# Layer 0's last MLP group summed in HBM, the weight sums of every MLP unit on VectorE, and later copies of running sums

## The chip, the cores and the metric

The kernel runs on one core of a Trainium2 chip. The metric is the device time of one launch in microseconds; the figure for the kernel before is the median of three runs, 2134.29 us (2131.2 to 2135.48).

## The reference

Two residual layers over 1024 tokens of width 1024, in fp32. Each layer adds a token mixer beside a 4-head cross-attention into 256 memory tokens, through one output projection, and then a squared-ReLU MLP of inner width 4096:

```python
for layer in range(2):
    h = rms_norm(x, norm_mix[layer])
    if layer % 2 == 0:
        y_mix, xq = rglru_group(h, w_in_a, ...)      # gated linear recurrence
    else:
        y_mix, xq = fox_group(h, w_in_b, ...)        # causal attention with forget gates
    y_mem = memory_group(xq, mem, norm_mem[layer], w_mem_kv[layer], ...)
    x = x + jnp.concatenate([y_mix, y_mem], axis=-1) @ w_out[layer]
    x = x + jnp.square(jax.nn.relu(rms_norm(x, norm_mlp[layer]) @ w_mlp_in[layer])) @ w_mlp_out[layer]
```

## The kernel before

Activations lie transposed, features on the 128 partitions, tokens along the free axis, in two halves of 512 tokens (h = 0 and h = 1). Every fp32 operand is split into a rounded part and a rest (`hi`, `lo`), and each product is three matmuls, hi*hi, hi*lo and lo*hi (`t3`). ScalarE writes `hi` (L316 for weights, L474 and L468 for activations), VectorE writes `lo` (L317, L477, L469). The residual stream x lies in HBM as `xs` (`xspill` in the trace) as eight blocks of 128 features.

The MLP of a layer runs in eight groups of 512 inner features. A group has two matrix products, `mlp_z` (first weight, w1) and `mlp_out` (second weight, w2), and each is done by a Winograd form of the 2x2 block product: seven block products instead of eight, in the order b11, b21, t2, t3, t1, t4, b22. Each is a call of `product` (matmuls at L1017, 24 of them on 512 columns). The price is sums of blocks. On the weight side these are a unit's S2 sums in `_wunit` (L355, L356, L357, twice each on 128x512, and L360 once on 128x1024), made on GpSimd, save that the first w1 unit of each layer makes them on VectorE (`u.dve = g == 0`). There are 8 w1 units and 8 w2 units in a layer.

On the activation side one PSUM bank collects several products in turn: A takes b11, then t2 on top of it, then t1, then b22; C takes t3 and then t4. A bank's running sum after b11, t2 and t3 is copied by ScalarE (`copies`, L1028) into an SBUF tile as soon as that product is done, and VectorE adds the other addend, another bank, when that is there (`plus`, L1033). In `mlp_z` the result goes through relu, scale and square (L1037, L1038), and combinations of the four blocks (L1138 to L1149) become operands of `mlp_out`. In `mlp_out` each of the 16 results of a group is added to `xs` in HBM by an accumulating DMA from GpSimd's queue (`send`, L1172).

The last group (g == 7) of both layers does otherwise: it reads x, adds it in SBUF, on GpSimd (L1192) or by an accumulating DMA into SBUF (L1195), and stores the finished x from SP's queue (`sink`, L1177). In layer 0 `sink` also squares the block for the next norm's statistics (`sqacc`, L438 and L444), and for h = 0 splits it for layer 1's projections (L468, L469). The key and value projection of layer 1's memory tokens (`kv`, matmuls at L385) starts before that group ends (two steps from `hook7`), and goes on after it.

All scratch tiles of 128x512 come from one set of 86 slots (`Slots`); the slot that was given back longest ago is taken first, and an instruction that writes a slot waits until its former reader, a DMA too, has ended. Weights go through four raw buffers and a ring of three split entries, `wnext` splitting up to three entries ahead. The order of the instructions on each engine is made at build time by a scheduler that goes by the program's order and its own model of durations.

In layer 1, groups 0 to 2 have their first two products done ahead (`mlp_park`) and read the results back, four tiles each, in the group before (`mlp_back`).

Of the kernel before, what the change touches and what calls it, by code (L numbers as in the profile page):

```python
# [175 lines left out]
class Builder:  # L176
# [712 lines left out]
    def outproj(self, h, ks, src, dst, gain, last, banks=("pj",)):  # L889
        nc = self.nc  # L890
        for m in range(8):
            x = self.load_x(m, h, src)
            wh, wl = self.wnext()
            ps = self.psum(banks[m % len(banks)])
            terms = []
            for i, k in enumerate(ks):
                c = slice(i * P, (i + 1) * P)
# [134 lines left out]
    def plus(self, f, ps):  # L1032
        self.nc.vector.tensor_tensor(f[:, :H], f[:, :H], ps, ALU.add)  # L1033

# [38 lines left out]
    def mlp_z(self, l, g, hook):  # L1073
# [19 lines left out]
        t, t2, w = [], [], []  # L1093
# [12 lines left out]
        else:  # L1106
            yield from run(A, "b11", True, self.copies(t))
            for o in range(2):
                hz[o]["b11"] = t[o]
# [43 lines left out]
    def mlp_out(self, l, g, mid):  # L1153
        nc = self.nc
        V, G = nc.vector, nc.gpsimd
        n = slice(0, H)
        hp = self.hp
        seen = set()
# [15 lines left out]

        def sink(f, q, a, b):
            x, dm = f[:, n], 2 * q + a
            nc.sync.dma_start((self.out if l else self.xs)[dm, :, b * H:(b + 1) * H], x)  # L1177
            if l == 0:
                self.sqacc(1 if b in seen else 0, b, x, V if b == 0 and a == 1 else None)
                seen.add(b)  # L1180
                if b == 0:
                    self.xg[0][dm] = self.split(x, self.pc("gmix1", dm))
            self.F.put(f)

        def keep(a, b):
            dst = []

            def first(q, ps):
                self.copies(dst)(q, ps)
                if g == 7 and a == b == 0:  # L1190
                    f = self.acc.pop(0)
                    G.tensor_tensor(dst[q][:, n], dst[q][:, n], f[:, n], ALU.add)  # L1192
                    self.F.put(f)
                elif g == 7:
                    nc.gpsimd.dma_start(dst[q][:, n], self.xs[2 * q + a, :, b * H:(b + 1) * H], accum_op=ALU.add)  # L1195

            def then(q, ps):
                self.plus(dst[q], ps)
                (sink if g == 7 else send)(dst[q], q, a, b)

            return first, then

        def end(q, ps):
            if g == 7:
                self.plus(acc[q], ps)
                sink(acc[q], q, 0, 1)
# [7 lines left out]
        c11, c21, c22 = keep(0, 0), keep(1, 0), keep(1, 1)  # L1214
# [576 lines left out]
```

## Time and profile before

| | |
|---|---|
| median of three runs | 2134.29 us |
| the profiled execution | 2132.37 us, its span 2130.7 us |
| TensorE matmul / weight load | 97% / 81% of the span |
| VectorE, ScalarE, GpSimd | 78%, 54%, 41% |
| mean granted TensorE clock | 0.988 of full speed |

The profile's page gives busy shares over the span; the table by stretch gives the same for windows, with the number of instructions (x), the granted clock, the share of the DMA engines and GB/s. A matmul record lasts longer than the distance to the next one, since matmuls are pipelined: 117 matmuls on 512 columns that start in 27 us are 0.231 us apart. In the views of waits each row has the engine and line that waited, what ended the wait, the us in total, the number of waits and the longest.

### The profile page before, as it was taken

How to read it: one execution, taken by the hardware profiler on the slowest of the kernel's cores; microseconds unless marked ns; L12 is line 12 of the kernel's file. 1: busy time of each engine (PE TensorE's matmuls, PEld its weight loads, DVE VectorE, ACT ScalarE, POOL GpSimd, SP SyncE). 2: the span in 40 equal slices, each digit the busy share in tenths (PEclk: the TensorE clock that was granted, in tenths of full speed). 3: DMA queues.
4: the chain of work that ended last, by engine and by line, in shares of the span. 5: the costliest groups of instructions: out<-in, count | busy, mean ns of one | idle time of the engine just before them, and what ended most of it. 6: DMA issues, size and time to landing. Idle time of an engine off the chain costs nothing. (4 is left out here: it accounts for less than half of the span.)

```text
span 2130.7 us, 30055 instructions
## 1 busy us (share of the span) xinstructions
PE 2071.5 (97%) x10466; PEld 1727.4 (81%) x10466; DVE 1663.3 (78%) x2708; ACT 1141.9 (54%) x2160; POOL 864.0 (41%) x844
## 2 busy tenths in 40 slices
PE   9999999999999999988999999999999999999998
PEld 8898878878778778767998998777777877787786
DVE  7988698877877877887677778776787768868777
ACT  6755655544454454555555646566544554445443
POOL 2222321535535525545342333422054645445444
PEclk8999999999999999989999999999999999999999
DMA  5422452546545635627768446934546675364474
GB/s 180 140 77 93 135 184 94 101 89 128 101 97 119 111 87 119 156 86 199 276 218 290 133 138 214 299 122 129 161 99 139 138 150 101 85 140 94 89 173 119
DMA packets 126392, 298.44 MB, mean 140 GB/s; under 512 B 14176, under 2 KB 16288, under 8 KB 126240
## 3 DMA queue, kind: packets, MB, share of 16 engines
q1 hardware_dynamic: 82464, 208.36, 29.4%
q0 software_dynamic: 43776, 88.17, 23.2%
q8 instruction: 82, 1.34, 0.3%
q14 instruction: 70, 0.57, 0.1%
HBM read 187.32 MB, written 109.15 MB: 139 GB/s over the span
## 5 line engine op out<-in xcount | busy, mean ns | idle before, releaser
L317 DVE TENSOR_TENSOR wl<-wr,wh 128x1024 fp32r<-128x1024 f32 (+2 forms) x362 | 441.2, 1229 | 108.5 <-ACT wh L316 104.1
L1017 PE MATMUL pspt<-r,wh 128*128 128x512 f32 x1536 | 485.1, 396 | 7.2 <-DVE r L477 2.6
L1172 POOL DMA_DIRECT2D xspill<-f x224 | 284.7, 1963 | 287.5 <-DVE f L1033 284.1
L316 ACT ACTIVATE wh<-wr 128x1024 fp32r<-128x1024 f32 (+3 forms) x411 | 306.0, 766 | 141.4 <-PE pss L1017 41.2
L1017 PEld LDWEIGHTS pspt<-r,wh 128*128 128x128 f32 x1536 | 289.0, 188 | 77.9 <-DVE r L477 4.3
L1017 PE MATMUL pss<-r,wh 128*128 128x512 f32 x1024 | 329.6, 400 | 19.8 <-ACT f L1028 8.1
L477 DVE TENSOR_TENSOR r<-f,r 128x512 fp32r<-128x512 f32 x282 | 230.1, 826 | 98.5 <-ACT r L474 39.9
L1017 PE MATMUL pspt<-r,wl 128*128 128x512 f32 x768 | 305.6, 398 | 0.2
L1017 PE MATMUL pspj<-r,wh 128*128 128x512 f32 x832 | 265.8, 399 | 2.1 <-DVE f L1033 1.0
L1017 PEld LDWEIGHTS pss<-r,wh 128*128 128x128 f32 x1024 | 192.6, 189 | 75.9 <-DVE r L477 13.9
L385 PE MATMUL pspj<-wh,r 128*128 128x256 f32 (+1 forms) x1280 | 248.5, 286 | 2.3 <-DVE r L1322 0.8
L474 ACT ACTIVATE r<-f 128x512 fp32r<-128x512 f32 x282 | 173.5, 626 | 106.2 <-DMA xspill<-f 49.0
L1038 ACT ACTIVATE f<-f 128x512 f32<-128x512 f32 x128 | 80.9, 632 | 269.5 <-DVE f L1037 269.4
L385 PEld LDWEIGHTS pspj<-wh,r 128*128 128x128 f32 x1280 | 201.6, 188 | 5.3 <-DVE r L1322 1.0
L1017 PE MATMUL pss<-r,wl 128*128 128x512 f32 x512 | 203.6, 398 | 0.0
L355 POOL TENSOR_TENSOR wr<-wr,wr 128x512 f32<-128x512 f32 x60 | 95.7, 1778 | 249.0 <-DVE wl L317 233.2
L1017 PEld LDWEIGHTS pspj<-r,wh 128*128 128x128 f32 x832 | 156.3, 189 | 39.4 <-DVE r L469 1.5
L385 PE MATMUL pspj<-wl,r 128*128 128x256 f32 (+1 forms) x640 | 181.1, 283 | 0.0
L1017 PEld LDWEIGHTS pspt<-r,wl 128*128 128x128 f32 x768 | 146.0, 190 | 36.9 <-DVE wl L317 2.0
L385 PE MATMUL pspj<-r,wh 128*128 128x512 f32 x488 | 164.1, 411 | 5.3 <-ACT r L474 2.1
L1017 PE MATMUL pspj<-r,wl 128*128 128x512 f32 x416 | 163.4, 397 | 0.6 <-DVE wl L317 0.5
L357 POOL TENSOR_TENSOR wr<-wr,f 128x512 f32<-128x512 f32 x60 | 135.4, 2550 | 17.1 <-issue 17.1
(301 smaller groups left out, 4035.3 us busy)
## 6 DMA issues: line engine op xcount, KB each, us to landing
wr<-in_w_dram SPq DMA_DIRECT2D x136, 512.0 KB, 4.5
xspill<-f POOLq DMA_DIRECT2D x224, 256.0 KB, 7.0
f<-xspill SPq DMA_DIRECT2D x88, 256.0 KB, 4.1
xspill<-f SPq DMA_DIRECT2D x64, 256.0 KB, 3.5
f<-in_xT_dram SPq DMA_DIRECT2D x32, 256.0 KB, 3.5
wr<-in_wkv_dram SPq DMA_DIRECT2D x16, 512.0 KB, 3.6
wr<-in_wina_dram SPq DMA_DIRECT2D x15, 512.0 KB, 3.6
wsp<-wh SPq DMA_DIRECT2D x14, 512.0 KB, 5.4
```

The source lines that it names most:

```text
L316: self.wact = self.nc.scalar.activation(hi, raw, AF.Copy)
L317: eng.tensor_tensor(lo, raw, hi.bitcast(F32), ALU.subtract)
L355: G.tensor_tensor(r["a11"][:, d], r["a11"][:, d], r["a21"][:, d], ALU.subtract)
L357: G.tensor_tensor(r["a12"][:, d], r["a12"][:, d], x, ALU.subtract)
L385: self.lastmm = self.nc.tensor.matmul(out, lhsT=a, rhs=b, start=(j == 0), stop=(j == n - 1))
L474: i = self.nc.scalar.activation(hi[:, :n], src, AF.Copy)
L477: self.nc.vector.tensor_tensor(lo[:, :n], src, hi[:, :n].bitcast(F32), ALU.subtract)
L1017: self.lastmm = self.nc.tensor.matmul(ps, lhsT=a, rhs=b, start=(start and c == 0 and j == 0), stop=(c == n - 1 and j == 2), skip_group_che ...
L1038: self.lastsq = self.nc.scalar.activation(f[:, n], f[:, n], AF.Square)
L1172: nc.gpsimd.dma_start(self.xs[2 * q + a, :, b * H:(b + 1) * H], f[:, n], accum_op=ALU.add)
```

## The change

Five edits, in one diff:

1. Every unit, w1 and w2, makes its S2 sums on VectorE.
2. Running sums are copied later. `both` copies one bank and adds the other at once, so that A after b11 is copied in b21's `done`, A after t2 in t3's, and C after t3 is not copied in `mlp_z` (VectorE reads it from PSUM in t1's `done`), and is copied in t1's `done` in `mlp_out`.
3. Layer 0's last group is like every other group: 16 accumulating DMAs to `xs`. Only layer 1's last group adds x in SBUF, now on VectorE for two of the four blocks.
4. Layer 1's first operand comes back from HBM: after six more steps of `kv`, `norm_split_back` loads the eight blocks of h = 0, splits them behind the last weight split, and takes their squares' sum on TensorE (`sq_pe`, four matmuls of one column for each block). `xq_proj` has done four steps before the norm is finished. For h = 1 the squares are taken in `norm_split`, their sums on GpSimd.
5. The weights of layer 1's output projection are loaded and split as 1024 columns for two blocks instead of 512 for one.

```diff
-    def split(self, xt, g, n=H):
+    def split(self, xt, g, n=H, behind=None):
         hi, lo = self.R.get(), self.R.get()
         self.last_hi = self.nc.scalar.activation(hi[:, :n], xt, AF.Copy, scale=g)
+        if behind is not None:
+            self.after(self.last_hi, behind)
...
+    def norm_split_back(self, h, g, src):
+        xs = self.xg[h] = [None] * 8
+        for j, k in enumerate((0, 2, 4, 6, 1, 3, 5, 7)):
+            x = self.load_x(k, h, src)
+            xs[k] = self.split(x[:, :H], self.pc(g, k), behind=self.wact)
+            self.sq_pe(j, h, x[:, :H], self.last_hi)
+            self.F.put(x)
+            yield
...
-            u.dve = g == 0
-            self.plan_unit("w2", 8 * l + g)
+            u.dve = True
+            u = self.plan_unit("w2", 8 * l + g)
+            u.dve = True
...
+    def both(self, pa, pb):
+        f = self.F.get()
+        self.nc.scalar.activation(f[:, :H], pa, AF.Copy)
+        self.plus(f, pb)
+        return f
...
         def c11(o, ps):
-            self.plus(hz[o]["b11"], ps)
-            self.relu2(hz[o]["b11"], hz[o]["b11"][:, n], 0)
+            f = hz[o]["b11"] = self.both(A[o], ps)
+            self.relu2(f, f[:, n], 0)
...
-        yield from run(A, "t2", False, self.copies(t2))
+        yield from run(A, "t2", False, None)
         C = [self.psum("s") for _ in range(2)]
-        yield from run(C, "t3", True, self.copies(w))
+        yield from run(C, "t3", True, lambda o, ps: self.copies(t2)(o, A[o]))
...
         def c22(o, ps):
-            self.plus(w[o], ps)
-            self.relu2(w[o], w[o][:, n], 1)
-            hz[o]["b22"] = w[o]
+            f = hz[o]["b22"] = self.both(ps, C[o])
+            self.relu2(f, f[:, n], 1)
...
+        last = l == 1 and g == 7
...
+        def pair(banks, a, b):
+            def done(q, ps):
+                f = self.both(banks[q], ps)
+                if last:
+                    x = xin[a, b][q]
+                    V.tensor_tensor(f[:, n], f[:, n], x[:, n], ALU.add)
+                    self.F.put(x)
+                (sink if last else send)(f, q, a, b)
+            return done
...
+        def u2(q, ps):
+            self.copies(dst)(q, A[q])
...
-        yield from run(A, "b11", True, c11[0])
-        yield from run([self.psum(k) for k in more], "b21", True, c11[1], "t3")
+        yield from run(A, "b11", True, None)
+        yield from run([self.psum(k) for k in more], "b21", True, pair(A, 0, 0), "t3")
         mid()
-        yield from run(A, "t2", False, c21[0], "t1")
+        yield from run(A, "t2", False, None, "t1")
...
-        yield from run(C, "t3", True, c22[0], "t4")
-        yield from run(A, "t1", False, c22[1], "b22")
-        yield from run(C, "t4", False, c21[1])
+        yield from run(C, "t3", True, u2, "t4")
+        yield from run(A, "t1", False, pair(C, 1, 1), "b22")
+        yield from run(C, "t4", False, c21)
...
-        self.plan += [self.ent("wout1m", m, 512, 1) for m in range(8)]
+        self.plan += [self.ent("wout1m", m, 1024, 1) for m in range(4)]
...
-        advance(kv, 5)
+        advance(kv, 6)
+        weave(kv, self.norm_split_back(0, "gmix1", self.xs), 1.0)
+        self.vst = {}
+        xq = self.xq_proj(0, 1)
+        advance(xq, 4)
         self.norm_fin(0, False, self.lastmm)
-        drain(kv)
-        self.vst = {}
-        drain(self.xq_proj(0, 1))
-        self.norm_fin(1, False)
+        drain(xq)
...
-        weave(self.fox_proj(0, 1), self.norm_split(1, "gmix1", self.xs, False), 0.5)
+        weave(self.fox_proj(0, 1), self.norm_split(1, "gmix1", self.xs, True), 0.5)
+        self.norm_fin(1, False)
```

## Rows read from the trace of the kernel before

**Rows 1.** The page: span, and the busy time of each engine.

```profile
span 2130.7 us, 30055 instructions
PE 2071.5 (97%) x10466; PEld 1727.4 (81%) x10466; DVE 1663.3 (78%) x2708; ACT 1141.9 (54%) x2160; POOL 864.0 (41%) x844
```

**Rows 2.** The table by stretch, below its line of columns: one turn from `mlp_z` to `mlp_out` in layer 0, three stretches of the passage from layer 0 to layer 1, one of the first group of layer 1's MLP, and the last group's turn in layer 1.

```profile
core 0: us, PE busy (x) PEld busy (x) DVE busy (x) ACT busy (x) POOL busy (x), PEclk, DMA share, GB/s
679.00:706.00 27.00, 27.00 (x117) 21.78 (x116) 24.04 (x28) 13.45 (x22) 11.77 (x7) 1.00 0.06 19
...
940.00:950.00 10.00, 5.22 (x16) 3.35 (x15) 10.00 (x11) 3.77 (x6) 5.87 (x4) 0.72 0.00 0
950.00:960.00 10.00, 7.15 (x20) 4.59 (x19) 10.00 (x15) 7.24 (x12) 3.47 (x4) 0.60 0.39 133
1000.00:1010.00 10.00, 10.00 (x65) 10.00 (x65) 9.04 (x32) 6.30 (x19) 6.28 (x7) 0.71 0.61 207
1560.00:1570.00 10.00, 6.11 (x21) 4.56 (x20) 10.00 (x12) 5.15 (x9) 5.75 (x5) 0.78 0.28 59
...
2073.00:2100.00 27.00, 23.36 (x96) 18.28 (x96) 26.97 (x25) 13.33 (x23) 19.61 (x11) 0.96 0.00 0
```

**Rows 3.** What TensorE waited for: the first row is of the whole span; the next two are the first and the last of the ten rows for 930 to 1012 us, with the second between them; the last two are all that stands for 2066 to 2130 us.

```profile
PE pss L1017 <- ACT f L1028: 8.1, 3, 3.9
...
PE pspt L385 <- DVE wl L317: 3.7, 2, 2.6
PE pspt L1017 <- DVE r L477: 2.6, 1, 2.6
...
PE pso L378 <- DVE f L444: 0.3, 1, 0.3
...
PE pss L1017 <- DVE r L477: 3.1, 1, 3.1
PE pss L1017 <- ACT r L474: 0.6, 1, 0.6
```

**Rows 4.** Single lines over the whole span: one of the sums on GpSimd (count, busy us, mean ns), then VectorE instructions with minimum, median and maximum duration in ns: two of the sums in the first units, the activation split with two SBUF inputs, and the same line with one input from PSUM.

```profile
L355 POOL TENSOR_TENSOR wr<-wr,wr 128x512 f32<-128x512 f32 x60 | 95.7, 1778 | 249.0 <-DVE wl L317 233.2 <-DMA wr<-in_w_dram 15.7
...
L355 DVE TENSOR_TENSOR wr<-wr,wr x4: 680/682/692, 332.5 to 1441.7; 128x512 f32<-128x512 f32 x4
L360 DVE TENSOR_TENSOR wr<-wr,wr x2: 1207/1212/1218, 338.6 to 1513.2; 128x1024 f32<-128x1024 f32 x2
L477 DVE TENSOR_TENSOR r<-f,r x282: 670/682/2885, 20.6 to 2105.0; 128x512 fp32r<-128x512 f32 x141
L477 DVE TENSOR_TENSOR r<-pspt,r x48: 665/681/693, 144.7 to 1280.6; 128x512 fp32r<-128x512 f32 x48
```

**Rows 5.** VectorE's costliest groups by line and shape in 684.5 to 706 us, a turn from `mlp_z` to `mlp_out` (count, busy us, mean ns, idle before).

```profile
L317 DVE TENSOR_TENSOR wl<-wr,wh 128x1024 fp32r<-128x1024 f32 x3 | 5.8, 1950 | 0.0
L477 DVE TENSOR_TENSOR r<-f,r 128x512 fp32r<-128x512 f32 x4 | 4.4, 1109 | 0.0
L1037 DVE SCALAR_TENSOR_TENSOR f<-f,f 128x512 f32<-128x512 f32 x2 | 2.8, 1396 | 0.0
L317 DVE TENSOR_TENSOR wl<-f,wh 128x512 fp32r<-128x512 f32 x2 | 2.1, 1064 | 0.0
```

**Rows 6.** VectorE in order of time at the end of the same stretch (start us, us): two instructions on 512 columns that follow each other, the last activation split of t2's operand, and a split of 1024 columns with the one behind it.

```profile
698.13 0.68 DVE L1138 TENSOR_TENSOR f<-f,f 128x512 f32<-128x512 f32 x1
698.73 0.68 DVE L1037 SCALAR_TENSOR_TENSOR f<-pspt,f 128x512 f32<-128x512 f32 x1
...
704.75 0.68 DVE L477 TENSOR_TENSOR r<-f,r 128x512 fp32r<-128x512 f32 x1
...
705.96 1.21 DVE L317 TENSOR_TENSOR wl<-wr,wh 128x1024 fp32r<-128x1024 f32 x1
707.09 0.67 DVE L477 TENSOR_TENSOR r<-f,r 128x512 fp32r<-128x512 f32 x1
```

**Rows 7.** GpSimd in order of time in the same stretch: the first and the last of the four rows of a w2 unit's sums.

```profile
684.67 3.00 POOL L355 TENSOR_TENSOR wr<-wr,wr 128x512 f32<-128x512 f32 x2 [17.59 <-DVE wl L317]
...
694.67 2.99 POOL L357 TENSOR_TENSOR wr<-wr,f 128x512 f32<-128x512 f32 x2 [1.22 <-issue]
```

**Rows 8.** VectorE in order of time where the second half of t1 ends in that group's `mlp_z`: the add to C's copy, and the idle time before it.

```profile
682.03 0.69 DVE L1033 TENSOR_TENSOR f<-f,pspt 128x512 f32<-128x512 f32 x1 [1.44 <-PE pspt L1017]
```

**Rows 9.** What ScalarE's copies waited for between 1712 and 1722 us, and the accumulating sends: duration of the issue on GpSimd, and their count, size and median us from issue to landing.

```profile
ACT f L1028 <- DMA xspill<-f: 5.3, 1, 5.3
...
L1172 POOL DMA_DIRECT2D xspill<-f x224: 842/1597/4876, 391.7 to 2051.5; - x112
...
xspill<-f POOLq DMA_DIRECT2D x224, 256.0 KB, 7.0
```

**Rows 10.** The passage between the layers in order of time: `kv`'s splits on VectorE, and x added on GpSimd; then, over the whole span, the activation split with a gain on ScalarE and the one-column matmuls.

```profile
932.23 5.52 DVE L590 SCALAR_TENSOR_TENSOR r<-f,par,r 128x256 fp32r<-128x256 f32 x4
938.27 3.10 DVE L590 SCALAR_TENSOR_TENSOR r<-f,par,r 128x256 fp32r<-128x256 f32 x4
...
939.58 6.29 POOL L1192 TENSOR_TENSOR f<-f,f 128x512 f32<-128x512 f32 x4 [0.70 <-ACT f L1028]
...
L468 ACT ACTIVATE r<-f,par 128x512 fp32r<-128x512 f32 x56 | 39.7, 717 | 34.5 <-DMA f<-xspill 21.1 <-POOL f L444 5.6 <-issue 3.7
L462 PE MATMUL pso<-cD,f 128*128 128x1 f32 x192 | 27.5, 267 | 0.5 <-ACT f L449 0.5
```

More of the change, by code (lines that the diff above doesn't have):

```diff
@@ L890, in outproj @@
         nc = self.nc
+        per = 8 // len(ks)
         for m in range(8):
             x = self.load_x(m, h, src)
-            wh, wl = self.wnext()
+            if m % per == 0:
+                wh, wl = self.wnext()
             ps = self.psum(banks[m % len(banks)])
@@ L896, in outproj @@
             for i, k in enumerate(ks):
+                i += m % per * len(ks)
                 c = slice(i * P, (i + 1) * P)
@@ L1089, in c11 @@
         def c11(o, ps):
[L1090 to L1093 removed]
+            f = hz[o]["b11"] = self.both(A[o], ps)
+            self.relu2(f, f[:, n], 0)
+        t2 = []
         if g in self.parked:
@@ L1106, in mlp_z @@
         else:
-            yield from run(A, "b11", True, self.copies(t))
-            for o in range(2):
-                hz[o]["b11"] = t[o]
+            yield from run(A, "b11", True, None)
             yield from run([self.psum("pj") for _ in range(2)], "b21", True, c11)
-        yield from run(A, "t2", False, self.copies(t2))
+        yield from run(A, "t2", False, None)
         C = [self.psum("s") for _ in range(2)]
-        yield from run(C, "t3", True, self.copies(w))
+        yield from run(C, "t3", True, lambda o, ps: self.copies(t2)(o, A[o]))
         hp["b11"] = [self.split_sb(hz[o]["b11"][:, n]) for o in range(2)]
         def c22(o, ps):
-            self.plus(w[o], ps)
-            self.relu2(w[o], w[o][:, n], 1)
-            hz[o]["b22"] = w[o]
+            f = hz[o]["b22"] = self.both(ps, C[o])
+            self.relu2(f, f[:, n], 1)
         yield from run(A, "t1", False, c22)
@@ L1154, in mlp_out @@
         nc = self.nc
-        V, G = nc.vector, nc.gpsimd
+        V = nc.vector
         n = slice(0, H)
         hp = self.hp
-        seen = set()
         def run(banks, key, start, done, ahead=None):
@@ L1173, in send, with c21 @@
             self.F.put(f)
+        last = l == 1 and g == 7
         def sink(f, q, a, b):
[L1176 to L1182, printed above, removed]
-            self.F.put(f)
[L1185 to L1201, printed above, removed]
+            nc.sync.dma_start(self.out[2 * q + a, :, b * H:(b + 1) * H], f[:, n])
+            self.F.put(f)
+        def pair(banks, a, b):
[7 more added lines that the diff above has]
+            return done
+        dst = []
+        def c21(q, ps):
+            self.plus(dst[q], ps)
+            (sink if last else send)(dst[q], q, 1, 0)
+        def u2(q, ps):
+            self.copies(dst)(q, A[q])
+            if last:
+                nc.gpsimd.dma_start(dst[q][:, n], self.xs[2 * q + 1, :, :H], accum_op=ALU.add)
         def end(q, ps):
-            if g == 7:
-                self.plus(acc[q], ps)
-                sink(acc[q], q, 0, 1)
+            if last:
+                x = xin[0, 1][q]
+                self.plus(x, ps)
+                sink(x, q, 0, 1)
             else:
@@ L1213, in mlp_out @@
         more = ("pt", "pt", "pt", "o")
-        c11, c21, c22 = keep(0, 0), keep(1, 0), keep(1, 1)
-        yield from run(A, "b11", True, c11[0])
-        yield from run([self.psum(k) for k in more], "b21", True, c11[1], "t3")
+        xin = {(0, 0): self.acc} if last else {}
+        yield from run(A, "b11", True, None)
+        yield from run([self.psum(k) for k in more], "b21", True, pair(A, 0, 0), "t3")
         mid()
-        yield from run(A, "t2", False, c21[0], "t1")
+        yield from run(A, "t2", False, None, "t1")
         C = [self.psum(k) for k in more]
-        acc = [self.load_x(2 * q, 1, self.xs) for q in range(4)] if g == 7 else None
-        yield from run(C, "t3", True, c22[0], "t4")
-        yield from run(A, "t1", False, c22[1], "b22")
-        yield from run(C, "t4", False, c21[1])
+        for k in ((1, 1), (0, 1)) if last else ():
+            xin[k] = [self.load_x(2 * q + k[0], k[1], self.xs) for q in range(4)]
+        yield from run(C, "t3", True, u2, "t4")
+        yield from run(A, "t1", False, pair(C, 1, 1), "b22")
+        yield from run(C, "t4", False, c21)
         yield from run(A, "b22", False, end)
@@ L1238, in hook7 @@
                 advance(nxt)
-            if key == "t1":
+            if key == "t1" and l:
                 self.acc = [self.load_x(2 * q, 0, self.xs) for q in range(4)]
@@ L1537, in run @@
         self.plan_fox(1)
-        self.plan += [self.ent("wout1x", m, 512, 1) for m in range(8)]
-        self.plan += [self.ent("wout1m", m, 512, 1) for m in range(8)]
+        self.plan += [self.ent("wout1x", m, 1024, 1) for m in range(4)]
+        self.plan += [self.ent("wout1m", m, 1024, 1) for m in range(4)]
         for g in TUNE["park"]:
@@ L1543, in run @@
             self.plan_unit("w1", 8 + g, Unit.ALL[:1])
-        self.plan += [self.ent("wout1x", m, 512, 1) for m in range(8)]
+        self.plan += [self.ent("wout1x", m, 1024, 1) for m in range(4)]
         self.plan_mlp(1, TUNE["park"], TUNE["wait"])
@@ L1732, in _pack @@
         o[nme] = st(C(w[ks].reshape(-1, D)))
+        if len(ks) == 4:
+            o[nme] = C(o[nme].reshape(4, 2, P, 512).transpose(0, 2, 1, 3).reshape(4, P, 1024))
     w1, w2 = [], []
```

1 line of the change is left out of this document (removed).

## The prediction

> **What bounds the kernel now.** I read the page's busy shares first. TensorE is busy for 97% of the span [rows 1], and its matmuls hardly change in number, so what the change can give is bounded by the time in which TensorE stands or runs slowly. The table by stretch says where that is. In a turn inside layer 0's MLP TensorE is busy for all of 27.00 us, with 117 matmuls, one in 0.231 us, at a granted clock of 1.00 [rows 2]: there is nothing to win but much to lose. In the passage between the layers it starts 16 matmuls in one stretch of 10 us and 20 in the next, where the pace gives 43, and the clock falls to 0.72 and 0.60, a mix of its two levels, 1.2 and 2.4 GHz, behind those gaps; it is 0.71 again at 1000 us. The first group of layer 1's MLP shows the same on a smaller scale (21 matmuls, 0.78), and the last group's turn holds 96 matmuls instead of 117. VectorE is busy for 9.04 to 10.00 of 10 us in the four short stretches and 26.97 of 27 in the last.
>
> The view of waits names what TensorE waits for there: 8.1 us in all for ScalarE's copies of running sums (three waits, all in layer 1's MLP), 16.2 us in ten rows from 3.7 down to 0.3 in the passage (nearly all end with VectorE), 3.1 and 0.6 us in the last turn [rows 3]. So the view of VectorE's single lines comes next. A split with two inputs in SBUF takes 670 to 682 ns as a rule and up to 2885; the same line with an input from PSUM never takes over 693 [rows 4]. The long ones stand beside GpSimd's sums [rows 5, 7]. VectorE is late because GpSimd works.
>
> **The change part by part.**
>
> *Sums on VectorE.* Before, 30 units of 32 make them on GpSimd (60 instructions of L355 for 30 units [rows 4]). On VectorE a unit has six instructions on 512 columns and one on 1024. Successive starts lie 0.60 us apart for the one (698.13, 698.73) and 1.13 for the other (705.96, 707.09) [rows 6], the durations 0.68 and 1.21 us being those of the first units [rows 4]. So a unit adds 6 x 0.60 + 1.13 = 4.7 us to VectorE, 30 of them 142 us. What it takes away is read in a turn: eleven instructions with two SBUF inputs last 5.8 + 4.4 + 2.8 + 2.1 = 15.1 us [rows 5], and alone would last 3 x 1.21 + 8 x 0.68 = 9.1. The saving is 6.0 us, in the stretch from 684.67 to 697.7 in which GpSimd sums [rows 7]. Net, VectorE gets 1.3 us less to do in each turn, and its 24.04 us of 27 [rows 2] become some 22.7. The turn is where it matters: t2's operand is split at 704.75 [rows 6], when TensorE wants it, so each us there counts whole. TensorE's waits in a turn are tenths of a us, so the gain ends quickly; I take 2 us over all. From below: if the scheduler lays sums ahead of the splits and nothing is saved, a turn costs 4.7 us, and there are 15 more or less equal ones. From above: VectorE's whole excess in the last turn goes, below. The w1 units' sums fall into `mlp_out`, with no such chain behind them; there an in-order VectorE may stand before a raw weight that has not landed, where GpSimd stood before (15.7 us on weights in all [rows 4]); other work on VectorE waits behind it, and I put nothing on it as the ends of that (0 and 15.7) lie nearer to 0 while the splits are three entries ahead.
>
> A rule speaks against this part. The Trainium skill (Perfetto Trace Analysis, Optimizing Scalar/DVE Operations) says that where VectorE is saturated, moving work to ScalarE or even GpSimd may make sense, and adds that the shared port may spoil the latter. By its first half the sum would be 15 turns x 4.7 us = 70 us slower, which is the lower end above; by its second half it is the sum I make. The trace bears out the second: 2885 ns against 693.
>
> *Late copies.* The number of copies hardly falls: the same tiles are filled later. What falls is how long slots are held: in `mlp_out` four tiles less in b11, t2 and t3, in `mlp_z` two less. The slot shortage is seen at 1717 us, where a copy waits 5.3 us for a send of the group before that takes 7.0 us to land [rows 9]. All three waits of TensorE for a copy (8.1 us [rows 3]) are of this kind, at 1562, 1648 and 1717 us, in the first groups of layer 1, when parked tiles hold slots as well. The copy of b11 is now asked for one product, 24 x 0.231 = 5.6 us, later. I count 7 of 8.1 as gone, and 1 more for the clock of 0.78 behind the first of them [rows 2]. What is late next is TensorE itself.
>
> The new price: banks are held longer. In `mlp_z`, t4's first matmul may now start on C only after ScalarE has copied A and VectorE has read C. Behind t1's first half there are twelve matmuls of its second half, 2.8 us, against about 0.6 for the copy and 0.69 for the add; VectorE stands idle for 1.44 us before that add [rows 8]. So it is covered by some 1.4 us. With the cover gone every turn would wait twice; bounds are 0 and 2 x 0.69 x 16 = 22 us. I take 2, nearer to 0 because of the idle time.
>
> *The last group.* In layer 1 GpSimd no longer adds x in the turn; VectorE does, after b21, behind the chain. With the sums gone too, of the 3.7 us waited [rows 3] I take 3. The very end, an add and a store behind the last matmul, stays.
>
> *The passage.* The sixteen stores with their squares, adds on GpSimd (6.29 us for four) and eight splits leave the tail of the MLP. `kv`'s eight splits on VectorE stay; 256 columns take 5.52 + 3.10 us for eight beside GpSimd [rows 10]; alone I estimate 8 x 0.34 = 2.7, half of the 0.68 of 512 columns each. SP's queue has no stores that wait for VectorE between weight loads. The sixteen sends take 0.84 to 1.6 us each of GpSimd's queue [rows 9], ahead of GpSimd's share of `kv`'s weight splits. Of the 16.2 us waited I count half, 8, as gone, and a third of the 9.7 us that the clock took ((0.28 + 0.40 + 0.29) x 10 [rows 2]), so 11. It may be all 26, or none: the waits may only change their name. Against it stand 28 more one-column matmuls, 27.5 / 192 = 0.14 us each [rows 10], 4 us, and the way back of x. The even blocks were sent three products before the group's end, the odd ones one product (5.6 us) before it, landing 7.0 us after the issue; six steps of `kv` (72 matmuls on 256 columns) cover that. The eight splits and squares on ScalarE, 8 x (0.72 + 0.62) = 10.7 us, fit into the ten steps that are left only if weights don't crowd them; a wait of 0 to 5 us before `xq_proj`, I take 1. Net 6. ScalarE's and GpSimd's extra squares for h = 1 lie beside `fox_proj`, six or more steps before they are wanted: nothing.
>
> *Wider output weights.* Half the loads, twice the size, three entries ahead as before: nothing, within 1 us.
>
> The sum: 2 + 8 + 3 + 6 - 2 = 17 us less. Against the profiled execution's 2132.4 us that is 2115.4; the median of the runs is 1.9 us above that execution, so 2117.
>
> **The rivals.**
>
> A, *the passage gives nothing.* x comes back late, and TensorE stands before `xq_proj` instead of before `kv`. For it: the chip has 16 more accumulating transfers at 7.0 us each where DMA was at up to 0.61 [rows 2]. Against it: the distance of six steps. Time: 2134.3 - 11 = 2123.
>
> B, *VectorE becomes the bound in the turns.* The saving of 6.0 us exists only where GpSimd's sums lie beside VectorE's chain, but the 4.7 us are added for certain, and the scheduler may put them ahead of the chain. For it: VectorE full for 26.97 of 27 us in the last turn, and no slack at 704.75. It decides once a unit saves under 4.7 - 15 / 15 = 3.7 us, since every us counts fifteen times and the other parts give 15. With a saving of 3 us: 15 x 1.7 = 26 slower, less 15: 2145. Against it: the single rows, 6.0 us.
>
> C, *banks are held too long.* t4 waits for the add to C, 0.6 us twice in 16 groups, 19 us, which eats the gains: about 2134, no change.
>
> D, *the copies' waits change their name.* The change doesn't free slots in time, as layer 1's parked tiles still hold them, so the 8 us stay: with the rest 2125.
>
> **How the numbers follow.** The forecast 0.52, A 0.14, B 0.16, C 0.10, D 0.08. A difference under 0.2% (4.3 us) can't be told from none here. Faster: forecast, A, D and a fifth of C, 0.76. Same: half of C and little of B and the forecast's edge, 0.08. Slower: B and a third of C, 0.16. The forecast alone ranges from 2106 to 2126 (the passage at 15 or at 0, the banks at 0 or at 5). The range goes on to 2098, where the passage gives 25 us, and up to 2139, into C and the near side of B.
>
> **What would show each step right or wrong.** Right: L477 and L1037 with two SBUF inputs at 0.68 us in the turns; no wait of TensorE for L1028; over 30 matmuls in each 10 us from 940 to 1000, clock near 1. Wrong: 117 matmuls in 27 us no longer reached inside layer 0's MLP (B); TensorE waiting for L1033 at t4 (C); TensorE waiting for a split behind a load of x (A); copies still waiting for sends (D). The prediction falls if GpSimd's freedom shortens no VectorE row, or if layer 0's groups 1 to 6 grow by more than a us each.

## The result, and the profile after

The changed kernel takes 2121.82 us (median of five runs), before 2134.29: a ratio of 0.9944, 95% interval 0.993 to 0.9959. The forecast was 2117, in a range from 2098 to 2139. So the sign and most of the size came as forecast; the terms of the sum did not, and most of what follows is about them.

The page of the kernel after, the lines that answer to [rows 1], and the granted clock in 40 slices:

```profile
span 2120.2 us, 29851 instructions
PE 2073.9 (98%) x10522; PEld 1740.0 (82%) x10522; DVE 1575.7 (74%) x2910; ACT 1152.1 (54%) x2156; POOL 490.0 (23%) x611
...
PEclk8999999999999999999999999999899999999999
```

GpSimd lost 374 us of work, and VectorE, which took over 30 units of sums, has 88 us less to do; in the run with the sums alone, below, it has 69 less (1594.4 us) for 210 more instructions. Its instructions became shorter by more than the sums cost. The split of a weight's 512 columns with two SBUF inputs shows it (minimum, median and maximum ns over the span), before and after:

```profile
L317 DVE TENSOR_TENSOR wl<-f,wh x64: 673/890/4646, 342.2 to 2088.7; 128x512 fp32r<-128x512 f32 x64
```
```profile
L317 DVE TENSOR_TENSOR wl<-f,wh x64: 683/691/706, 344.7 to 2080.9; 128x512 fp32r<-128x512 f32 x64
```

In the trace of the kernel before, 590 VectorE instructions on 512 columns with two SBUF inputs overlap no GpSimd instruction that reads SBUF, and took 659 to 771 ns; the 221 that overlap one took 1172 ns in the median. TensorE has 56 more matmul records.

The table by stretch, below its line of columns, for the stretches that answer to [rows 2]: the passage, the first group of layer 1's MLP, and the last turn.

```profile
core 0: us, PE busy (x) PEld busy (x) DVE busy (x) ACT busy (x) POOL busy (x), PEclk, DMA share, GB/s
...
925.00:935.00 10.00, 10.00 (x45) 8.12 (x44) 10.00 (x16) 7.92 (x15) 2.34 (x2) 1.00 0.00 0
935.00:945.00 10.00, 6.02 (x22) 4.08 (x21) 10.00 (x14) 8.68 (x19) 3.92 (x3) 0.86 0.18 52
...
1560.00:1570.00 10.00, 4.98 (x14) 3.19 (x13) 10.00 (x16) 5.74 (x9) 1.83 (x2) 0.67 0.57 104
2077.00:2104.00 27.00, 26.97 (x117) 21.43 (x116) 26.40 (x40) 17.89 (x30) 3.59 (x4) 1.00 0.28 64
```

The last turn is whole: 117 matmuls in 27 us against 96. The passage still has a gap, though a shorter one. The first group of layer 1's MLP is worse than before, with 14 matmuls in 10 us against 21 (the table of lag below has 21.7 us there against 9.0).

What TensorE waited for, over the whole span, the first four rows:

```profile
PE pss L1032 <- ACT wh L316: 4.1, 1, 4.1
PE pss L1430 <- DVE mn L1435: 4.1, 3, 2.2
PE pspj L385 <- DMA wh<-wsp: 3.0, 3, 1.9
PE pspt L1032 <- ACT r L476: 2.9, 1, 2.9
```

The 8.1 us on copies [rows 3] are gone. The longest single wait that is left is for a weight split (L316) in layer 1's first group.

To see where time went I laid each trace's matmul records against a full pace (0.233 us from one start to the next on 512 columns, 0.118 on 256, 0.112 on one, as these rows stand in undisturbed stretches). What the trace takes beyond that is the time in which TensorE stood or ran slowly; I call it lag, and the time at full pace work. By stretch, in us, with the kernels of the experiments below (an e or x stands for an edit of the kernel after, a b for one of the kernel before; "turns" are groups 0 to 6 of layer 0; about 1 us at the very end is in no stretch):

```
                start  turns  passage attention first g1-3   g4-7   last | lag  work
                       L0     L0->L1  layer 1   group              turn |
before           24.8    5.3   25.8     25.1     9.0    7.8    1.7    5.9 | 106.5 2020.0
after            27.3   -0.1    9.5     27.8    21.7    2.3   -0.3    0.2 |  89.6 2026.3
e_sums_pool      26.8   22.7   13.6     30.0    21.8   14.2    8.0    2.8 | 140.8 2026.3
e_early_copies   25.2    0.8   10.0     26.8    17.9    0.1    0.1   -0.1 |  82.0 2026.3
e_passage        24.7    0.4   14.9     22.5    19.3    3.5    0.0    0.2 |  86.8 2020.0
e_wout512        25.3   -0.3   10.5     32.2     7.9    2.3   -0.3    0.3 |  79.5 2026.3
x_512_pass       24.1    0.0   15.0     26.1    11.2    2.7   -0.3    0.3 |  80.5 2020.0
x_512_early      24.7    0.5    8.5     33.1    11.3    0.4    0.1    0.0 |  79.6 2026.3
x_first_pool     25.7    0.4   11.6     28.4    19.8    9.2   -0.3    0.2 |  95.9 2026.3
b_sums           28.3    0.8   24.4     26.1    11.5    0.2    0.1    6.1 |  98.8 2020.0
b_vadd           28.7    6.4   23.4     22.3     9.0    8.0    2.0    5.3 | 106.5 2020.0
b_sums_vadd      24.9    0.6   25.1     23.1     8.5    0.0    0.1    4.3 |  87.5 2020.0
b_dummy_read     26.4   50.9   29.9     25.8    20.6   21.6   21.4   10.4 | 208.5 2020.0
b_dummy_write    24.5    2.6   24.1     27.4    16.1    1.2    0.2    4.5 | 101.8 2020.0
```

The start, about 335 us before the first MLP group, varies by 4.6 us among kernels whose edits hardly touch it; I read nothing from differences of a few us there. The kernel after stands 2.0 to 2.6 us longer in it than the three kernels that take out its copies, its passage or its wide weights, so that much of what each of them gains isn't placed by the table. The table is of one profiled execution for each kernel; with the sums back on GpSimd and with the sums alone it was the longest of the four, 8.1 and 4.1 us above the median. Of the change itself: lag 16.9 less, work 6.3 more, 10.6 us together, and 10.5 by the profiled spans (2130.7 to 2120.2).

### The profile page after: what moved, and what is told of

It is laid out like the page before. It is cut to its first block, busy times and chain, and to the rows that moved or that the text cites. A ratio compares the mean times of both kernels' runs of the same rounds, so it can differ in the third digit from the quotient of the medians.

```text
span 2120.2 us, 29851 instructions
## 1 busy us (share of the span) xinstructions
PE 2073.9 (98%) x10522; PEld 1740.0 (82%) x10522; DVE 1575.7 (74%) x2910; ACT 1152.1 (54%) x2156; POOL 490.0 (23%) x611
## 5 line engine op out<-in xcount | busy, mean ns | idle before, releaser
L317 DVE TENSOR_TENSOR wl<-wr,wh 128x1024 fp32r<-128x1024 f32 (+2 forms) x354 | 346.0, 987 | 238.3 <-ACT wh L316 235.5
L1032 PE MATMUL pspt<-r,wh 128*128 128x512 f32 x1536 | 497.0, 396 | 6.7 <-ACT r L476 2.9
L316 ACT ACTIVATE wh<-wr 128x1024 fp32r<-128x1024 f32 (+3 forms) x403 | 304.1, 776 | 289.9 <-PE pss L1032 114.5
L1189 POOL DMA_DIRECT2D xspill<-f x240 | 210.8, 998 | 832.8 <-DVE f L1048 799.7
L1032 PE MATMUL pspj<-r,wh 128*128 128x512 f32 x832 | 272.9, 402 | 3.9 <-DVE f L915 2.8
L479 DVE TENSOR_TENSOR r<-f,r 128x512 fp32r<-128x512 f32 x282 | 192.0, 696 | 60.8 <-DMA xspill<-f 41.1
L476 ACT ACTIVATE r<-f 128x512 fp32r<-128x512 f32 x282 | 170.2, 625 | 66.1 <-PE pss L1032 15.8
L385 PE MATMUL pspj<-r,wh 128*128 128x512 f32 x488 | 161.8, 408 | 5.8 <-DMA wh<-wsp 1.9
L385 PEld LDWEIGHTS pspj<-wl,r 128*128 128x128 f32 x640 | 120.5, 188 | 0.7 <-issue 0.2
L1032 PEld LDWEIGHTS pss<-r,wl 128*128 128x128 f32 x512 | 97.4, 190 | 23.7 <-issue 0.2
```

The lines of the kernel that those rows point to most:

```text
L316: self.wact = self.nc.scalar.activation(hi, raw, AF.Copy)
L317: eng.tensor_tensor(lo, raw, hi.bitcast(F32), ALU.subtract)
L385: self.lastmm = self.nc.tensor.matmul(out, lhsT=a, rhs=b, start=(j == 0), stop=(j == n - 1))
L476: i = self.nc.scalar.activation(hi[:, :n], src, AF.Copy)
L479: self.nc.vector.tensor_tensor(lo[:, :n], src, hi[:, :n].bitcast(F32), ALU.subtract)
L1032: self.lastmm = self.nc.tensor.matmul(ps, lhsT=a, rhs=b, start=(start and c == 0 and j == 0), stop=(c == n - 1 and j == 2), skip_group_che ...
```

## The experiments

Twelve kernels, each against the kernel before; behind each median stand its ratio to that kernel and the 95% interval. Each has its name of the table of lag in brackets.

**The sums back on GpSimd** (e_sums_pool)

```diff
-            u.dve = True
-            u = self.plan_unit("w2", 8 * l + g)
-            u.dve = True
+            u.dve = g == 0
+            self.plan_unit("w2", 8 * l + g)
```

> The changed kernel with the weight sums back on GpSimd (save each layer's first w1 unit), all else as changed. Theory 1 (GpSimd's sums stretch VectorE): splits with two SBUF inputs last up to 2.9 us again, each of layer 0's groups 2 to 7 is 0.6 us longer per turn, the last turn of layer 1 waits 3 us or more, VectorE's busy time is 60 to 100 us higher in spite of 142 us less work; time 2128 to 2136. Theory 2 (the sums' move gives back at the start of layer 1's MLP what it wins elsewhere, since VectorE stood 3.5 us before a weight that had not landed): the 3.5 us wait and ScalarE's 7.1 us behind it go, time 2118 to 2124.

2165.42 us, 1.0142 (1.0125 to 1.0159): 43.6 us slower than the kernel after, and above both ranges. VectorE's busy time rises by 59.5 us (1575.7 to 1635.2) though it has 210 instructions less, and the longest of the 64 weight splits takes 4635 ns, 706 in the kernel after. The turns of layer 0 stand for 2.1 to 3.6 us each, the first for 6.4. With the sums on GpSimd the other edits make the kernel slower than before.

**The sums alone, in the kernel before** (b_sums): the same lines the other way round.

> The kernel before with all weight sums on VectorE, nothing else of the change. Theory 1 (this one edit gives all of the gain: the turns, most of the passage and the last turn): each group of layer 0 from 1 to 6 stands 0.0 us instead of 0.6, the passage some 10 us less, layer 1's first group no worse than before; time 2103 to 2112. Theory 2 (the edits need each other, since the turns were slowest with GpSimd's sums and late copies): 2118 to 2130.

2120.43 us, 0.9943 (0.9925 to 0.9962). This one edit gives what all five give. The time lies in the second theory's range, but the edits don't need each other for it; the first theory was right on the turns and wrong on the passage and the last turn, which stay (24.4 and 6.1 us). The turns lose their lag (5.3 to 0.8 and 1.7 to 0.1), and so do layer 1's groups 1 to 3 (7.8 to 0.2), with the copies still made early: two of the three waits for copies [rows 3], those at 1648 and 1717 us, went with GpSimd's sums. The third is still there, in the first group:

```profile
PE pspt L1018 <- ACT f L1029: 3.1, 1, 3.1
```

**Copies at once, as before** (e_early_copies)

```diff
-        yield from run(A, "b11", True, None)
-        yield from run([self.psum(k) for k in more], "b21", True, pair(A, 0, 0), "t3")
+        yield from run(A, "b11", True, self.copies(dA))
+        yield from run([self.psum(k) for k in more], "b21", True, pair(dA, 0, 0), "t3")
...
-        yield from run(A, "t2", False, None, "t1")
+        yield from run(A, "t2", False, u2, "t1")
...
-        yield from run(C, "t3", True, u2, "t4")
-        yield from run(A, "t1", False, pair(C, 1, 1), "b22")
+        yield from run(C, "t3", True, self.copies(dC), "t4")
+        yield from run(A, "t1", False, pair(dC, 1, 1), "b22")
```

(and alike in `mlp_z`)

> The changed kernel with the running sums copied at once as before. Theory 1 (late copies free slots): copies wait for sends again near groups 1 and 2 of layer 1's MLP, 2 to 5 us of TensorE waits on the copy line, time 2124 to 2130. Theory 2 (the waits for sends went because GpSimd has no sums and sends earlier, not because of the copies): no such waits, 2120 to 2123. Theory 3 (late copies cost, since ScalarE's copy and VectorE's read now stand before the next product on the bank): 2112 to 2119.

2114.65 us, 0.9903 (0.9889 to 0.9918): 7.2 us faster than the kernel after. In this kernel the late copies cost, as the third theory has it; its reason, the next product on the bank, wasn't tried by itself. Groups 1 to 3 of layer 1 stand 0.1 us instead of 2.3, the first group 17.9 instead of 21.7. TensorE waits for no copy of a running sum.

**Layer 0's last group in SBUF again** (e_passage), its store from `sink` and the old order of `kv`; the adds of x keep their place in `pair`.

```diff
-        last = l == 1 and g == 7
+        last = g == 7
...
-        advance(kv, 6)
-        weave(kv, self.norm_split_back(0, "gmix1", self.xs), 1.0)
...
+        advance(kv, 5)
```

> The changed kernel with layer 0's last group summed in SBUF, squared and split as before. Theory 1 (the passage gives some 11 us by itself): 2130 to 2136, and 7 to 12 us more between the last turn of layer 0 and the first key projection of layer 1. Theory 2 (the passage was slow because of GpSimd's sums beside VectorE, and is now fast either way): 2120 to 2125.

2112.79 us, 0.9898 (0.9883 to 0.9913): 9.0 us faster than the kernel after, below both ranges. The passage stands 5.4 us longer (14.9), but the attention behind it 5.3 less, the first group 2.4 less, and TensorE has 6.3 us less of one-column matmuls. It also stands 10.9 us less in the passage than the kernel before, though x goes through SBUF as there: the HBM way isn't what took these 10.9 away.

**Output weights of 512 columns** (e_wout512)

```diff
-        self.plan += [self.ent("wout1m", m, 1024, 1) for m in range(4)]
+        self.plan += [self.ent("wout1m", m, 512, 1) for m in range(8)]
```

(all four places, and `outproj` takes one entry for each block)

> The changed kernel with the output projection's weights in 512 columns as before. In the changed kernel the stretch from layer 1's attention to its MLP's first group is some 15 us slower than before. Theory 1 (the wider loads do that: TensorE waits 3.0 us for them, 1.0 before, and the order around them changes): 2108 to 2117. Theory 2 (they do nothing; the loss is in the first MLP group): 2119 to 2124.

2109.84 us, 0.9885 (0.9867 to 0.9904): 12.0 us faster than the kernel after, in the first theory's range. The first group of layer 1's MLP stands 7.9 us instead of 21.7, but the attention stands 4.4 us longer. The two belong together: 7.3 of the 13.8 us lie ahead of the group's own products, from the last product that is done ahead to the next one; the kernel after begins it earlier (1495.0 us against 1505.6) and loses 8.2 us until the next, this one 0.9. Together the two stretches fall from 49.5 to 40.1 us. In the first group's turn itself the kernel after stands 10.7 us, this one 4.0. The table by stretch, first the kernel after, then this one, 22 us from where b21 of its `mlp_out` begins:

```profile
1555.50:1577.50 22.00, 15.24 (x50) 11.10 (x49) 17.87 (x29) 9.59 (x16) 2.69 (x3) 0.77 0.49 109
```
```profile
1551.70:1573.70 22.00, 19.10 (x79) 14.15 (x78) 17.95 (x28) 12.89 (x22) 3.53 (x4) 1.00 0.53 125
```

50 matmuls against 79, and the granted clock is 0.77 in the stretch with the gap, 1.00 here. What the waits around it say, first after, then this kernel:

```profile
PE pss L1032 <- ACT wh L316: 4.1, 1, 4.1
...
DVE wr L355 <- DMA wr<-in_w_dram: 3.5, 1, 3.5
```
```profile
DVE wr L355 <- DMA wr<-in_w_dram: 3.8, 1, 3.8
...
PE pss L1030 <- DVE wl L317: 1.6, 1, 1.6
```

In both VectorE stands before a raw weight, 3.5 and 3.8 us, so that wait isn't the difference; TensorE's wait for a weight split is, 4.1 against 1.6. Why the wide entries put that split later I didn't try; three entries ahead mean six blocks of the projection instead of three, and the order of the instructions differs for long before.

**The S2-first w1 units of groups 1 to 3 on GpSimd** (x_first_pool)

```diff
-            u.dve = True
+            u.dve = g == 0 or g not in parked + wait
             u = self.plan_unit("w2", 8 * l + g)
```

> The changed kernel with the sums of layer 1's units whose S2 comes first (groups 1 to 3 of w1) on GpSimd. Theory 1 (VectorE's 3.5 us wait for a weight and the 7.1 us of ScalarE behind it cost TensorE in layer 1's first group): those waits go, 2112 to 2117. Theory 2 (that group was late before it, because of the second w2 sum at 1567 us that waits for a slot): 2119 to 2124.

2125.41 us, 0.9965 (0.9952 to 0.9978): 3.6 us more than the kernel after (ten runs from 2120.9 to 2132.0, so the two can't be told apart by time), and above both ranges. The first group still stands 19.8 us, and groups 1 to 3 go from 2.3 to 9.2. What TensorE waits for in these three groups, all rows:

```profile
PE pspt L1032 <- DVE wl L317: 5.6, 2, 3.1
PE pspt L1032 <- ACT pspt L1122: 1.5, 1, 1.5
```

So VectorE's wait for a raw weight isn't a price worth avoiding by this means: the theory that it cost the first group fell, and three units on GpSimd brought waits back in the groups that they serve.

**Two pairs: 512 columns with the old passage (x_512_pass), and with early copies (x_512_early)**

> The changed kernel with 512-column output weights and the old passage; sums on VectorE and late copies stay. If the undone edits' gains of 12 and 9 us are separate places (the first group of layer 1's MLP, and the 56 one-column records in the passage), they add: 2098 to 2104. If both come from one place, the order of instructions at the start of layer 1's MLP that any edit shakes up, they don't: 2108 to 2114.

> The changed kernel with 512-column output weights and the copies at once as before. Separate places: 2101 to 2106. One place: 2108 to 2114.

With the old passage 2106.52 us, 0.9874 (0.9859 to 0.989): the lowest median of the study, the change without its edits 3 (of layer 0), 4 and 5. It lies between the two ranges: the gains of 12.0 and 9.0 us give 15.3 together. With early copies 2112.93, 0.9902 (0.9873 to 0.993; four runs from 2106.8 to 2116.7), in the range of one place: not told from 512 columns alone, and the lags are the same (79.6 and 79.5). The gain of the early copies is shown beside wide weights only.

**x added on VectorE, in the kernel before** (b_vadd; with the sums too, b_sums_vadd)

```diff
-                    G.tensor_tensor(dst[q][:, n], dst[q][:, n], f[:, n], ALU.add)
+                    V.tensor_tensor(dst[q][:, n], dst[q][:, n], f[:, n], ALU.add)
```

> The kernel before with the last group's add of x on VectorE instead of GpSimd, and nothing else. My theory: the passage gains about 10 us (25.8 to some 15), the last turn about 3 of 5.9, since GpSimd's sums of that group's w2 unit still lie there: 2121 us, 2118 to 2125. Rival: with the sums on GpSimd the adds only move the lateness from GpSimd to VectorE: 2130 us or more.

> The kernel before with two edits only: every unit's S2 sums on VectorE, and the last group's add of x on VectorE instead of GpSimd. My theory: nearly all of the change's gain comes from taking GpSimd's instructions away from beside VectorE's chain, in the turns and in the passage; neither the later copies nor the way through HBM nor the wide output weights add to it. From the run with the sums alone (2120.4 us) I take off 9.5 us for the passage (24.4 to about 15 us stood there) and 5.9 us for the last turn (6.1 to about 0.2): 2105 us, 2102 to 2109. Rival: the passage's gain needs the way through HBM or the later copies: 2115 to 2121 us, with 24 us stood in the passage.

Alone 2130.81 us, 0.999 (0.998 to 1.0): no change. With the sums 2115.48, 0.9919 (0.9905 to 0.9933): 5 us less than the sums alone, 10 more than I expected. My theory fell: the passage stands 25.1 us, the last turn 4.3. The rival's time is right, and of its two reasons the way through HBM is out (the run with the old passage). The traces tell more of what is left. VectorE in order of time in the passage, with sums and adds on VectorE:

```profile
937.97 0.68 DVE L1193 TENSOR_TENSOR f<-f,f 128x512 f32<-128x512 f32 x1
938.58 0.68 DVE L477 TENSOR_TENSOR r<-f,r 128x512 fp32r<-128x512 f32 x1
939.18 0.68 DVE L1193 TENSOR_TENSOR f<-f,f 128x512 f32<-128x512 f32 x1
...
942.73 0.67 DVE L1193 TENSOR_TENSOR f<-f,f 128x512 f32<-128x512 f32 x1
943.33 1.27 DVE L477 TENSOR_TENSOR r<-f,r 128x512 fp32r<-128x512 f32 x2
...
949.87 0.68 DVE L477 TENSOR_TENSOR r<-f,r 128x512 fp32r<-128x512 f32 x1
```

and in the kernel with the old passage and the adds in `pair` (L479 is the same split, L1210 the add of x):

```profile
943.35 3.09 DVE L479 TENSOR_TENSOR r<-f,r 128x512 fp32r<-128x512 f32 x5
...
948.76 0.68 DVE L1048 TENSOR_TENSOR f<-f,pso 128x512 f32<-128x512 f32 x1
949.36 0.68 DVE L1210 TENSOR_TENSOR f<-f,f 128x512 f32<-128x512 f32 x1
```

`mlp_out` of that group begins at 925.5 and 925.2 us in the two kernels, and each makes 14 such splits around it. Where x is added to b11's copy, the four adds stand among and in front of the splits that the next products want, and the adds of b21 do too; the last row shown is the eleventh split, while in the other kernel the thirteenth is done by 946.4. TensorE's waits for the split in the passage, with sums and adds on VectorE:

```profile
PE pss L1018 <- DVE r L477: 5.4, 2, 4.6
PE pspt L1018 <- DVE r L477: 4.3, 1, 4.3
```

9.7 us; the other kernel has no wait for L479 there, and waits 4.7 us for ScalarE's part of the split (L476).

The last turn stands 4.3 us here and 0.2 with the adds in `pair`. The kernel with early copies stands -0.1 us there with its adds of x behind b21. VectorE around t2's product, first with sums and adds on VectorE (t2 begins at 2075.6 us), then with early copies (2080.6 us; L1206 is the add of x):

```profile
2068.97 1.28 DVE L1193 TENSOR_TENSOR f<-f,f 128x512 f32<-128x512 f32 x2
...
2083.26 2.49 DVE L477 TENSOR_TENSOR r<-f,r 128x512 fp32r<-128x512 f32 x4
```
```profile
2079.31 2.49 DVE L479 TENSOR_TENSOR r<-f,r 128x512 fp32r<-128x512 f32 x4
...
2087.66 1.28 DVE L1206 TENSOR_TENSOR f<-f,f 128x512 f32<-128x512 f32 x2
```

So in the last turn neither the time of the copies nor GpSimd or VectorE as the adder decides (6.1 us with the adds on GpSimd, 4.3 on VectorE); what is left is the place of the adds, though no run moved them alone. One more thing differs: (1,1) gets x by a load instead of an accumulating DMA into SBUF, for which VectorE waits 6.6 us in all in the last turn; but the first of these DMAs is issued at 2088.98 us, and the turn's lag lies between 2075 and 2086.

In the passage the place of the adds wasn't tried apart from the late copies, and the copies change the order there too: with late copies VectorE makes three more of the splits before `kv`'s eight, with early ones `kv`'s come first, and TensorE has lost 3.0 us against 6.1 when t2 begins. This can't be all, as with the HBM way, where no x is added in the passage, early copies stand 10.0 us and late ones 9.5. So the rows, the waits and this pair speak for the adds, but it isn't shown that they alone make the 10 us.

**Work on GpSimd that nobody waits for** (b_dummy_read, b_dummy_write). Both kernels are the one with sums and adds on VectorE, with GpSimd kept busy behind each unit's sums:

```diff
         G.tensor_tensor(r["a21"], r["a21"], r["a22"], ALU.add)
+        for _ in range(14):
+            self.nc.gpsimd.tensor_tensor(self.dm, r["a11"][:, :256], r["a11"][:, 512:768], ALU.subtract)
```
```diff
         G.tensor_tensor(r["a21"], r["a21"], r["a22"], ALU.add)
+        for _ in range(30):
+            self.nc.gpsimd.memset(self.dm, 0.0)
+        self.nc.gpsimd.tensor_tensor(self.dm, r["a11"][:, :256], r["a11"][:, 512:768], ALU.subtract)
```

> As the run with sums and adds on VectorE, and GpSimd gets, behind each unit's sums, 14 subtractions of 256 columns that read two pieces of the raw weight in SBUF and write a tile that nobody reads; no result waits for them but the raw buffer's next load. My theory (GpSimd's reads stretch VectorE's instructions that have two SBUF inputs): L477 and L317 with two SBUF inputs go over 1 us again where they stand, the turns of layer 0 stand 0.6 us or more per group again, 5 to 20 us in all: 2110 to 2125 us. Rival (the sums on GpSimd cost because their results come late, not because they disturb VectorE): no result comes later here, so 2105 us as without them, at most 2107.

> The same, with 30 memsets of 256 columns on GpSimd instead of 13 of the 14 subtractions, the one subtraction behind them: GpSimd is busy as well, and holds the raw buffer and its own queue (the sends too), but hardly reads SBUF. My theory: VectorE's rows stay at 0.68 and 1.21 us, the time at that of the kernel without them, 2105 us, at most 2108. Rival (what costs is that GpSimd's queue is full, so that sends or raw buffers are late): as slow as the run with the subtractions.

With the reads 2233.33 us, 1.0473 (1.0457 to 1.0489), 117.9 more than without; with the writes 2127.14, 0.9973 (0.996 to 0.9985), 11.7 more. VectorE's split of 512 columns with two SBUF inputs (min/median/max ns over the span): without either, then with the reads, then with the writes.

```profile
L317 DVE TENSOR_TENSOR wl<-f,wh x64: 675/682/694, 342.3 to 2067.8; 128x512 fp32r<-128x512 f32 x64
```
```profile
L318 DVE TENSOR_TENSOR wl<-f,wh x64: 674/1225/1707, 348.1 to 2186.5; 128x512 fp32r<-128x512 f32 x64
```
```profile
L318 DVE TENSOR_TENSOR wl<-f,wh x64: 671/679/693, 342.4 to 2081.8; 128x512 fp32r<-128x512 f32 x64
```

And the two groups on GpSimd (count, busy us, mean ns):

```profile
L363 POOL TENSOR_TENSOR dm<-wr 128x256 f32<-128x256 f32 x448 | 510.6, 1140 | 340.1 <-DVE wr L356 279.1 <-issue 33.0
```
```profile
L363 POOL MEMSET dm<- 128x256 f32 x960 | 353.1, 368 | 49.1
```

GpSimd's reads stretch VectorE's instruction to 1225 ns in the median, its writes leave it at 679. VectorE's busy time rises by 190.2 us with the reads (1589.8 to 1780.0) and by 11.4 with the writes. The Trainium skill (SBUF — State Buffer, Who interferes with whom) says just that: a VectorE instruction with two inputs from SBUF contends with a GpSimd instruction that reads SBUF, not with one that only writes. The trace agrees. What TensorE waited for most with the reads, over the whole span, is VectorE's split:

```profile
PE pss L1021 <- DVE r L480: 47.3, 16, 4.6
PE pspt L1021 <- DVE r L480: 13.3, 5, 8.9
```

That reads cost is settled; its size I had far too low (117.9 us for 5 to 20), since with the sums on VectorE a turn has no room for them (VectorE is busy for 26.33 of 27 us in one, 605 to 632 us, without the reads): layer 0's seven turns stand 50.9 us, 7.3 each, and layer 1's later ones as much. That writes are free I had wrong too, though the rival, as slow as the reads, is far off: in the first group of layer 1 the lag is 16.1 us instead of 8.5. There memsets stand among the accumulating sends in GpSimd's queue, ScalarE stands 11.1 us (5.8 without the memsets) before a slot that a send still reads, and TensorE waits for a copy again:

```profile
PE pss L1022 <- ACT f L1033: 6.2, 1, 6.2
```

## Why the prediction was right, and where it was wrong

- *Sums on VectorE, -2.* Right in kind: the weight splits with two SBUF inputs are at 683 to 706 ns in the kernel after (up to 4646 before, the same line), and VectorE's total fell. The term was mis-sized: the sums alone gave 13.5 us (2133.9 to 2120.4). I counted TensorE's waits in the turns as ending quickly; by lag they were 5.3 us in layer 0 and 1.7 in layer 1's groups 4 to 7, and with the sums alone 0.8 and 0.1 are left. The same step also removed most of what I gave to the next one. In the turn of [rows 2] VectorE is no emptier (24.74 of 27 us with the sums alone, not the 22.7 reckoned), but makes 37 instructions instead of 28.
- *Late copies, -8.* Wrong. I read all three waits for a copy as waits for sends; two were (4.2 of 8.1 us), and both went through the step above, as the run with the sums alone has early copies and neither of them. The copy of the third, 3.9 us at 1562, stood behind VectorE's weight split for 2.4 us and behind no send; with the sums alone it is still 3.1, and the first group in which it lay stands longer in the kernel after, on other waits (21.7 against 9.0). That GpSimd's queue held the sends up before fits the run with the memsets, where work ahead of the sends brings a wait for a copy back; it wasn't tried by itself. The late copies cost 7.2 us in this kernel.
- *Banks held, +2.* No wait of TensorE at t4 shows in a turn of the kernel after; 0.
- *Last turn, -3.* 5.9 to 0.2. I named the place of the add ("after b21, behind the chain") and put the gain on GpSimd's freedom as well; the sums alone leave 6.1, and the runs point to the place.
- *Passage, -6 net.* The net is about 5 by the lags (16.3 less in the passage, against 6.3 of work and 5.3 of standing in the attention behind it, by the run that takes the edit out), from other parts than I had. The gross gain of 11 came, but not from the HBM way: 25.8 to 14.9 with the old way of x, with the late copies and the moved adds. The way through HBM took 5.4 more from the passage and cost 14 elsewhere. The sign "over 30 matmuls in each 10 us from 940 to 1000" came from 950 on (44 and more, clock 1.00); from 940 to 950 there are 19, clock 0.66. Of "28 more one-column matmuls, 4 us" there are 56 records and 6.3 us (64 more of the sums of squares, 8 fewer elsewhere). "Extra squares for h = 1 ... nothing" stands against the 5.3 us behind the passage, which go with this edit; which of its parts makes them stays open.
- *Wide output weights, 0.* Wrong: 12.0 us. "Three entries ahead as before" should have made me look, since the same count of entries is twice the blocks; that this is how the 12.0 us arise wasn't tried.

The rivals: A (2123) and D (2125) each gave a time within a few us of the measured one, for reasons that the traces deny (the passage gained; the copies' waits went). B didn't come, as the single rows had it; the run with reads shows a kernel in which VectorE is the bound of the turns. C is denied by the turns (-0.1 us).

The rule that I weighed against the sums (Perfetto Trace Analysis, Optimizing Scalar/DVE Operations, in the Trainium skill: offloading from VectorE to GpSimd may make sense, or the shared port may spoil it) comes out by its second half, by 43.6 us in this kernel.

So the sum came within 5 us by luck, since errors of both signs met: the sums and, as far as is shown, the order of the adds gave some 30 us of lag (turns, layer 1's groups 1 to 7, passage by 10.9, last turn), against which the kernel after gave back 19 us in work and in the other stretches, where the late copies, the HBM way and the wide weights each cost. The edits' prices aren't additive: the late copies cost 7.2 us with wide weights and nothing that can be told without them.

## What to carry to other kernels

A wait that ends with VectorE is read further than its releaser: first whether GpSimd reads SBUF beside it, then which instructions of lesser urgency stand before it in its queue. When several edits come in one diff, each is taken out by itself before one is believed: here one of them gave the whole net gain by itself, a change of order that came along with another went with some 16 us, and three gave that back. A prefetch counted in entries changes its reach when the entries grow; 12.0 us went with that here, by a way that stays open.

## What the runs showed of the hardware that I had not expected

GpSimd pays as well: 418 of its subtractions of 256 columns overlap a VectorE instruction with two SBUF inputs and took 1072 ns in the median; the 30 that overlap none took 732 to 762 (GpSimd's spans are rough in the profile). And 510.6 us of reads that nobody needs cost 117.9 us of the kernel's time, though VectorE was busy for only 80% of that span: in a turn it has no slack to give.
